# One TensorE branch per gate, up and down matrix, and weight splits of 2048 columns in three buffers

## The chip, the cores and the metric

The kernel runs on one core of one Trainium2 chip. The metric is the device time of one execution in microseconds (us). Three runs of the kernel before gave 1469.05, 1475.29 and 1476.32 us; their median is 1475.29 us.

## The reference: what is computed

A two-layer transformer trunk in float32: 256 tokens, width 1024. Each layer has a hybrid token mixer (latent attention, retention and block-sparse attention, fed by one input projection and joined by one output projection) and a channel mixer, each followed by a layer norm with a scaled residual. The channel mixer of layer 0 is a dense SwiGLU of width 2816. That of layer 1, on which this change works, is a mixture of eight SwiGLU experts with two experts for each token:

```python
logits = xt @ w_router
top_v, top_i = lax.top_k(logits, 2)
top_w = softmax(top_v)
gates = sum(one_hot(top_i, 8) * top_w[..., None], axis=1)
for e in range(8):
    y = y + gates[:, e:e+1] * (silu(xt @ w_gate[e]) * (xt @ w_up[e])) @ w_down[e]
```

Per expert, gate and up are 1024 x 3584 and down is 3584 x 1024, all float32. The weights of the eight experts are 352 MB, and all of them are read in every execution.

## The kernel before, in words

**Precision by splits.** TensorE works on a reduced float32 (F32R). Each weight tile is split into a high part `whi` (ScalarE's cast, line 152) and a low part `wlo` (VectorE's subtraction, line 153; for five early splits partly on GpSimd), and each product is three matmuls: high by high, high by low, low by high (`mm3`, lines 162 to 164). `split` makes one pair for up to 1024 columns, in a pool of `SPL` = 5 buffers for `whi` and 5 for `wlo` that lives through the whole kernel.

**Raw weights.** SyncE's queue loads the weights in pieces of 128 x 2048 (1 MB, line 122). In the expert stage `mchunk` takes the pieces' buffers from three pools in the cyclic order `ORDER`: 12 of them, and one more early piece (`EARLY`) in a buffer that a later gather uses. A load is issued when its buffer is free, that is, when VectorE has done the subtraction on what was there.

**The expert stage** goes over expert e = 0 to 7 and, in each, over m = 0 to 6, 56 blocks in all. A block multiplies the tokens of the expert (at most 128 slots, gathered by matmuls) by 512 columns of gate and of up, and 512 rows of down. The order on TensorE is: gate of this block, transposes of the hidden rows `hh` of the block before (`turn`), up of this block, down of the block before. Gate, up and down are 4096 columns each, so each is four splits of 1024.

**Heavy and light.** From expert 1 on, the count of the expert's tokens decides at run time. With more than 64 tokens the block runs `heavy`: three matmuls per product. With 64 or fewer it runs `light`: the high and the low part of the tokens stand side by side in the 128 columns of the stationary operand, so two matmuls do, and the two halves of the result are folded together by one more matmul (`fold`, line 838). For the fold, ScalarE first copies the bank to `fl` (line 850). `either` writes this as an If with an Else on TensorE alone. Before the change each of gate, up and down has two such branches, one per two splits, and the folds are Ifs of their own (`folded`, line 837): one after the first half of up (for gate) and one after the first half of the next down (for up). So a block has eight Ifs. Expert 0 has none, it is always heavy.

**What is put between the splits.** `defer(n, fn)` runs `fn` after n more splits of 1024: the copy to `fl` (`FOLD_N`), ScalarE's silu on the gate bank (line 894, `SILU_N`), the high and low part of the transposed rows (`halves`, lines 922 and 924, `HT_N`) and VectorE's product of silu and up (line 900, `MULT_N`). Within that, the framework's scheduler orders the instructions of each engine ahead of time, by when it thinks that they are ready, so a deferred one may stand a few splits later in its engine's queue than in the program. Each engine then works through its queue in order.

**Before the first expert.** `hold_splits` gives the first splits of expert 0 to VectorE or GpSimd and ties them behind certain instructions of the layer norm and the router, so that five splits are made while the router runs.

Of the kernel before, what the change touches and what calls it, by code (L numbers as in the profile page):

```python
# [18 lines left out]
P = 128  # L19
D = 1024  # L20
# [14 lines left out]
EARLY = 12  # L35
# [9 lines left out]
ORDER = (0, 0, 0, 0, 1, 1, 1, 1, 1, 0, 0, 2)  # L45
LAST = (7, 6)
POOL_LO = ()
# [40 lines left out]
def trunk(ctx: ExitStack, tc: tile.TileContext, x, consts, mconsts, vecs, lnrows, w_in, w_uq, w_ukv, w_o,  # L88
# [5 lines left out]
    spl = ctx.enter_context(tc.tile_pool(name="spl", bufs=SPL))  # L94
# [543 lines left out]
    def moe(pool, raws2, raws3, r, gb, rw):  # L638
# [4 lines left out]
        def mchunk(src, parts=1):  # L643
            pools = []
            for _ in range(2):
                i = nchunk[0]
                nchunk[0] += 1
                pools.append((pool, "xg") if i == EARLY else (raws, raws2, raws3)[ORDER[(i - (i > EARLY)) % 12]])
            return chunk(src, 4096, pools=pools, parts=parts)
# [76 lines left out]
        def gather(pr):  # L726
            pm = pool.tile([P, 2, 256], F32R, tag="pm", name="pm")
            for tt in range(2):
                for j in range(2):
                    ip = nc.vector.tensor_scalar(pm[:, tt, j * P:(j + 1) * P], iota, posm[:, tt, 2 * pr + j:2 * pr + j + 1],  # L730
                                            None, ALU.is_equal)
            if pr == 0:
                hold_splits(((), None, 2), ((pw,), nc.gpsimd, 2), ((i1, pw), nc.gpsimd, 1), ((i1, ip), None, 4))
            xgs = [pool.tile([P, KD, P, 2], F32R, tag="xg", name="xg", bufs=3) for j in range(2)]

            def part(k2):
                for hl, src in enumerate((xth, xtl)):
                    b = bank(acc, "gx")
                    for kk in range(2):
                        k = 2 * k2 + kk  # L740
                        for tt in range(2):
                            nc.tensor.matmul(b[:, kk * 256:(kk + 1) * 256], src[:, tt, k * P:(k + 1) * P], pm[:, tt, :],
                                             start=(kk == 0 and tt == 0), stop=(kk == 1 and tt == 1))
                    bv = b.rearrange("p (a b) -> p a b", b=256)
                    for j in range(2):
                        o = xgs[j][:, 2 * k2:2 * k2 + 2, :, hl]
                        if j == 0:
                            nc.vector.tensor_copy(o, bv[:, :, 0:P])
                        else:
                            nc.scalar.copy(o, bv[:, :, P:256])  # L750

            return pm, xgs, part
# [45 lines left out]
        nsplit = [0]  # L798

# [5 lines left out]
        def msplit(src):  # L805
            i_ = nsplit[0]
            nsplit[0] += 1
            pool_lo = i_ % 12 in POOL_LO
            t = split(src, 1024, nc.gpsimd if pool_lo else nc.vector)
            if not pool_lo:  # L810
# [24 lines left out]
        def folded(e, b, fl):  # L835
            if few[e] is not None:
                with tc.If(few[e] != 0):  # L837
                    nc.tensor.matmul(b, fold, fl[0], start=False, stop=True, skip_group_check=True)

        def gate_up(e, m, xg, part=None, mid=None):  # L840
# [3 lines left out]
            if part:  # L844
                part(0)

            def copy_for_fold(g, fl):
                with after(last[0]):
                    fl.append(pool.tile([P, 512], F32R, tag="fl", name="fl"))
                    nc.scalar.copy(fl[0], bs[g])  # L850

            fls = [[], []]
            for g, w in enumerate((e_gate, e_up)):
                raw = mchunk(w[e, m], 2 if g == 1 and (e, m) == LAST else 1)
                for q in range(2):
                    if part and g == 0:
                        sp = []
                        for k in range(4 * q, 4 * q + 4):
                            if k % 2 == 0:
                                if k < 6:  # L860
                                    part(k // 2 + 1)
                                sp.append(msplit(raw(k * 512, 1024)))
                            cs = slice((k % 2) * 512, (k % 2 + 1) * 512)
                            mm3(bs[g], xg[:, k, :, 0], xg[:, k, :, 1], sp[-1][0][:, cs], sp[-1][1][:, cs], k == 0, k == 7)
                        continue
                    sp = [msplit(raw(k * 512, 1024)) for k in (4 * q, 4 * q + 2)]
                    parts_ = [(k, sp[k // 2 % 2][0][:, k % 2 * 512:k % 2 * 512 + 512],
                               sp[k // 2 % 2][1][:, k % 2 * 512:k % 2 * 512 + 512]) for k in range(4 * q, 4 * q + 4)]

                    def heavy():  # L870
                        for k, hi, lo in parts_:
                            mm3(bs[g], xg[:, k, :, 0], xg[:, k, :, 1], hi, lo, k == 0, k == 7)

                    def light():
                        for k, hi, lo in parts_:
                            x2 = xg[:, k, 0:64, :].rearrange("p a b -> p (a b)")
                            nc.tensor.matmul(bs[g], x2, hi, start=(k == 0), stop=False)  # L877
                            nc.tensor.matmul(bs[g], x2, lo, start=False, stop=(k == 7))  # L878

                    either(e, heavy, light)  # L880
                    if g == 1 and q == 0:
                        folded(e, bs[0], fls[0])
                if dyn:
                    if g == 0 or (e, m) != LAST:
                        defer(FOLD_N, lambda g=g: copy_for_fold(g, fls[g]))
                    else:
                        copy_for_fold(g, fls[g])
                if g == 0:
# [7 lines left out]
                    defer(SILU_N, silu)  # L896
# [5 lines left out]
            def fold_up():  # L902
                folded(e, bs[1], fls[1])
                if (e, m) == LAST:
                    mult()
# [5 lines left out]
            return hh, fold_up  # L911
# [20 lines left out]
        def down(e, m, ht, yb, fold_up=None, hook=None):  # L932
            raw = mchunk(e_down[e, m], 2 if e == NE - 1 and m >= FM - 2 else 1)
            for q in range(2):
                sp = [msplit(raw(j * D, D)) for j in (2 * q, 2 * q + 1)]

                def heavy():
                    for j in (2 * q, 2 * q + 1):
                        hi, lo = sp[j % 2]
                        for n in range(2):  # L940
                            cs = slice(n * 512, n * 512 + 512)
                            mm3(yb[n], ht[:, j, 0], ht[:, j, 1], hi[:, cs], lo[:, cs], m == 0 and j == 0, m == FM - 1 and j == 3)

                def light():
                    for j in (2 * q, 2 * q + 1):
                        h2 = ht[:, j].rearrange("p a b -> p (a b)")[:, 0:256:2]
                        for n in range(2):
                            for i in range(2):
                                nc.tensor.matmul(yb[n], h2, sp[j % 2][i][:, n * 512:n * 512 + 512],  # L949
                                                 start=(m == 0 and j == 0 and i == 0), stop=(m == FM - 1 and j == 3 and i == 1))  # L950

                either(e, heavy, light)
                if q == 0 and fold_up:
# [111 lines left out]
        def finish(e, m, ht, fold_up=None, hook=None):  # L1065
# [3 lines left out]
            down(e, m, ht, yb[e], fold_up, hook)  # L1069
# [5 lines left out]
        for e in range(NE):  # L1075
            pr = e // 2
            for m in range(FM):
# [11 lines left out]
                hh, fold_up = gate_up(e, m, half[pr][1][e % 2], half[0][2] if e == 0 and m == 0 else None, mid)  # L1089
# [5 lines left out]
                if prev is not None:  # L1095
                    h2 = [ht[0]]
                    finish(*prev[:2], ht[0], fold_up, (lambda: h2.append(turn(hh, 0, 1024))) if (e, m) == LAST else None)
# [29 lines left out]
    with tc.tile_pool(name="pre", bufs=1, reuse_waits="tile") as pre:  # L1127
# [112 lines left out]
    with tc.tile_pool(name="moe", bufs=1, reuse_waits="tile") as mp, tc.tile_pool(name="raws3", bufs=ORDER.count(2), reuse_waits="tile") as raws3, \  # L1240
# [114 lines left out]
```

## Time and profile before

| what | value |
|---|---|
| median of three runs | 1475.29 us |
| the profiled execution, its own time | 1477.69 us |
| span of the profiled execution, first to last instruction | 1475.7 us |
| granted TensorE clock, mean | 0.981 of full speed |
| busy share of the span: TensorE, VectorE, ScalarE, GpSimd | 94%, 82%, 70%, 5% |
| read from HBM | 426.76 MB |
| expert stage, from about 487 to 1465 us: TensorE, VectorE, ScalarE busy | 918.8, 889.9, 791.9 of 978 us |

The shares are means over stages with different limits. Matmuls are pipelined, so two that follow one another overlap in the records: the distance between their starts is the cost of one, and a busy TensorE may still have room. An instruction's idle time and what ended it stand in brackets behind it; where a wait had several causes, the one named is the one that came last.

### The profile page before, as it was taken

To read this page: it belongs to the slowest core of one execution; us is meant where nothing else is said; L and a number is where in the kernel's file an instruction comes from. 1 tells how busy PE (TensorE), PEld (TensorE's weight loads), DVE (VectorE), ACT (ScalarE), POOL (GpSimd) and SP (SyncE) were. 2 spreads that over 40 slices of the span, in tenths; PEclk is the share of its full clock that TensorE was granted. 3 is DMA by queue.
4 is the path that set the end of the run, shared out by engine and by line. 5 is a ranking of instruction groups with operands and counts; after the bars stand their busy time and mean duration, and the time that the engine had idled before them with its cause. 6 is when DMAs were issued, how large, how long until landed. Compare 5 with 4: busy or idle time off the path is not lost. (4 is left out here: it accounts for less than half of the span.)

```text
span 1475.7 us, 20166 instructions
## 1 busy us (share of the span) xinstructions
PE 1379.9 (94%) x6927; PEld 1115.9 (76%) x6927; DVE 1204.0 (82%) x1590; ACT 1035.0 (70%) x1391; POOL 76.4 (5%) x113
## 2 busy tenths in 40 slices
PE   7999999999998999989889999998999999999995
PEld 6987999998986888766666677776677877777663
DVE  6577655547668799899999988899998888888997
ACT  3564444444655677878979877788887777778894
POOL 3112000003104000000000000000000000000001
PEclk8999999999998899999999999999999999999998
DMA  6733555544527599999999998989999898889980
GB/s 245 282 143 114 200 178 194 181 164 141 208 94 306 195 340 367 356 359 348 421 373 406 417 343 316 347 332 396 414 376 341 324 346 306 333 347 359 355 349 31
DMA packets 63526, 429.59 MB, mean 291 GB/s; under 512 B 7058, under 2 KB 7570, under 8 KB 15268
## 3 DMA queue, kind: packets, MB, share of 16 engines
q1 hardware_dynamic: 63364, 427.81, 75.9%
q8 instruction: 84, 1.38, 0.4%
q14 instruction: 46, 0.38, 0.1%
q0 software_dynamic: 32, 0.03, 0.0%
HBM read 426.76 MB, written 1.05 MB: 290 GB/s over the span
## 5 line engine op out<-in xcount | busy, mean ns | idle before, releaser
L153 DVE TENSOR_TENSOR wlo<-raw,whi 128x1024 fp32r<-128x1024 f32 (+3 forms) x801 | 933.7, 1213 | 156.7 <-ACT whi L152 155.1
L152 ACT CAST whi<-raw 128x1024 fp32r<-128x1024 f32 (+4 forms) x808 | 808.9, 1042 | 216.6 <-PE gu L586 44.0
L878 PE MATMUL eg<-wlo,xg 128*128 128x512 f32 x448 | 186.5, 416 | 1.8 <-DVE wlo L153 1.5
L162 PE MATMUL eg<-whi,xg 128*128 128x512 f32 x448 | 180.5, 403 | 6.8 <-PEq L837 6.8
L877 PE MATMUL eg<-whi,xg 128*128 128x512 f32 x448 | 180.3, 402 | 0.1
L163 PE MATMUL eg<-wlo,xg 128*128 128x512 f32 x448 | 176.9, 395 | 2.0 <-DVE wlo L153 1.7
L164 PE MATMUL eg<-whi,xg 128*128 128x512 f32 x448 | 176.0, 393 | 0.0
L878 PEld LDWEIGHTS eg<-wlo,xg 128*128 128x128 f32 x448 | 84.5, 189 | 50.1 <-DVE wlo L153 33.4
L162 PEld LDWEIGHTS eg<-whi,xg 128*128 128x128 f32 x448 | 87.3, 195 | 29.3 <-issue 12.8
L949 PE MATMUL y<-wlo,wk 128*128 128x512 f32 x224 | 96.7, 432 | 12.7 <-DVE wlo L153 12.6
L163 PEld LDWEIGHTS eg<-wlo,xg 128*128 128x128 f32 x448 | 87.4, 195 | 18.2 <-DVE wlo L153 3.8
L164 PEld LDWEIGHTS eg<-whi,xg 128*128 128x128 f32 x448 | 87.4, 195 | 16.0
L585 PE MATMUL gu<-xhi,whi 128*128 128x256 f32 x352 | 99.3, 282 | 0.1
L586 PE MATMUL gu<-xlo,whi 128*128 128x256 f32 x352 | 99.2, 282 | 0.2 <-DVE xlo L225 0.2
L587 PE MATMUL gu<-xhi,wlo 128*128 128x256 f32 x352 | 98.9, 281 | 0.0
L877 PEld LDWEIGHTS eg<-whi,xg 128*128 128x128 f32 x448 | 85.0, 190 | 15.9 <-issue 1.1
L949 PE MATMUL y<-whi,wk 128*128 128x512 f32 x224 | 93.3, 417 | 3.1 <-DVE wk L924 2.2
L162 PE MATMUL y<-whi,wk 128*128 128x512 f32 x224 | 90.2, 403 | 5.1 <-PEq L837 4.2
L163 PE MATMUL y<-wlo,wk 128*128 128x512 f32 x224 | 88.8, 396 | 1.6 <-DVE wlo L153 1.5
L164 PE MATMUL y<-whi,wk 128*128 128x512 f32 x224 | 88.5, 395 | 0.0
L949 PEld LDWEIGHTS y<-wlo,wk 128*128 128x128 f32 x224 | 45.1, 201 | 37.9 <-DVE wlo L153 31.7
L894 ACT ACTIVATE hh<-eg 128x512 f32<-128x512 f32 x56 | 33.6, 600 | 53.3 <-PEq L837 28.3
(307 smaller groups left out, 2147.3 us busy)
## 6 DMA issues: line engine op xcount, KB each, us to landing
raw<-in_e_gate SPq DMA_DIRECT2D x112, 1024.0 KB, 6.7
raw<-in_e_up SPq DMA_DIRECT2D x110, 1024.0 KB, 6.8
raw<-in_e_down SPq DMA_DIRECT2D x108, 1024.0 KB, 6.4
raw<-in_ffn_gu SPq DMA_DIRECT2D x22, 1024.0 KB, 4.9
raw<-in_ffn_dn SPq DMA_DIRECT2D x11, 1024.0 KB, 4.6
raw<-in_w_in SPq DMA_DIRECT2D x10, 960.0 KB, 4.6
raw<-in_w_o SPq DMA_DIRECT2D x8, 1024.0 KB, 6.2
gb<-in_lnrows SPq DMA_DIRECT2D x8, 512.0 KB, 4.3
```

The costliest lines, as they stand in the source:

```text
L152: last[0] = nc.scalar.copy(hi[:, :n], src)
L153: last[1] = (eng or nc.vector).tensor_tensor(lo[:, :n], src, hi.bitcast(F32)[:, :n], ALU.subtract)
L162: nc.tensor.matmul(o, ahi, bhi, start=start, stop=False)
L163: nc.tensor.matmul(o, ahi, blo, start=False, stop=False)
L164: return nc.tensor.matmul(o, alo, bhi, start=False, stop=stop)
L585: nc.tensor.matmul(o, hi[:, cs], xhi[:, k, :], start=(g == 0 and k == 0), stop=False)
L586: nc.tensor.matmul(o, hi[:, cs], xlo[:, k, :], start=False, stop=False)
L587: nc.tensor.matmul(o, lo[:, cs], xhi[:, k, :], start=False, stop=(g == 1 and k == 7))
L877: nc.tensor.matmul(bs[g], x2, hi, start=(k == 0), stop=False)
L878: nc.tensor.matmul(bs[g], x2, lo, start=False, stop=(k == 7))
L894: nc.scalar.activation(hh, bs[0], AF.Silu)
L949: nc.tensor.matmul(yb[n], h2, sp[j % 2][i][:, n * 512:n * 512 + 512], start=(m == 0 and j == 0 and i == 0), stop=(m == FM - 1 and j == 3 a ...
```

## The change

`either` is now called once for gate, once for up and once for down, after both of its splits are issued. The fold of gate goes into the light branch of up, before its last two products, and the fold of up into the light branch of down, before its last row block; where that down belongs to the expert before (m = 0), the fold of up keeps an If of its own. `msplit` makes splits of 2048 columns, in a new pool `spl2` of three buffers that opens with the expert stage, where the pool of five is closed. The first block, the last up and the last two downs still work in instructions of 1024 columns. The raw buffers are 11 instead of 12 and the early piece is the 12th instead of the 13th. Silu and the product of an expert with a branch wait for one more split (of 1024, counted). The last product of silu and up moves from behind its fold to behind the down that contains it.

```diff
-EARLY = 12
+EARLY = 11
-ORDER = (0, 0, 0, 0, 1, 1, 1, 1, 1, 0, 0, 2)
+ORDER = (0, 0, 0, 0, 1, 1, 1, 1, 0, 0, 2)
...
-    def split(src, n, lo_eng=None):
-        hi = spl.tile([P, 1024], F32R, tag="whi", name="whi")
-        lo = spl.tile([P, 1024], F32R, tag="wlo", name="wlo")
+    spl = [None]
+
+    def split(src, n, lo_eng=None, to=None):
+        hi, lo = to or [spl[0].tile([P, 1024], F32R, tag=t, name=t) for t in ("whi", "wlo")]
...
-                hold_splits(((), None, 2), ((pw,), nc.gpsimd, 2), ((i1, pw), nc.gpsimd, 1), ((i1, ip), None, 4))
+                hold_splits(((), None, 2), ((pw,), nc.gpsimd, 2), ((i1, pw), nc.gpsimd, 1), ((i1, ip), None, 3))
...
+        def msplit(raw, o, halves=False, before=None):
+            t = [spl[0].tile([P, 2048], F32R, tag=x, name=x) for x in ("whi", "wlo")]
+            n = 1024 if halves else 2048
+            for c in range(0, 2048, n):
+                if before:
+                    before((o + c) // 1024)
+                split(raw(o + c, n), n, nc.vector, [x[:, c:c + n] for x in t])
                 dve[0] = last[1]
-            for q in list(later):
-                q[0] -= 1
-                if q[0] == 0:
-                    later.remove(q)
-                    q[1]()
+                for q in list(later):
+                    q[0] -= n // 1024
+                    if q[0] <= 0:
+                        later.remove(q)
+                        q[1]()
             return t
...
-        def folded(e, b, fl):
-            if few[e] is not None:
-                with tc.If(few[e] != 0):
-                    nc.tensor.matmul(b, fold, fl[0], start=False, stop=True, skip_group_check=True)
+        def fold_in(b, fl):
+            if fl:
+                nc.tensor.matmul(b, fold, fl[0], start=False, stop=True, skip_group_check=True)
...
+                def four(q):
+                    halves = (e, m) == (0, 0) or g == 1 and (e, m) == LAST
+                    sp.append(msplit(raw, q * 2048, halves, (lambda i: i < 3 and part(i + 1)) if part and g == 0 else None))
+
+                def light():
+                    for k in range(KD):
+                        if g == 1 and k == 6:
+                            fold_in(bs[0], fls[0])
+                        cs = slice(k % 4 * 512, k % 4 * 512 + 512)
+                        x2 = xg[:, k, 0:64, :].rearrange("p a b -> p (a b)")
+                        nc.tensor.matmul(bs[g], x2, sp[k // 4][0][:, cs], start=(k == 0), stop=False)
+                        nc.tensor.matmul(bs[g], x2, sp[k // 4][1][:, cs], start=False, stop=(k == 7))
+
+                if dyn:
+                    four(0)
+                    four(1)
                     either(e, heavy, light)
-                    if g == 1 and q == 0:
-                        folded(e, bs[0], fls[0])
+                else:
+                    for q in range(2):
+                        four(q)
+                        heavy(range(4 * q, 4 * q + 4))
...
-                    defer(SILU_N, silu)
+                    defer(SILU_N + dyn, silu)
...
-                defer(MULT_N, mult)
+                defer(MULT_N + dyn, mult)
...
+            if few[e] is not None:
+                sp.extend(msplit(raw, q * 2048, parts > 1) for q in range(2))
                 either(e, heavy, light)
-                if q == 0 and fold_up:
+            else:
+                for q in range(2):
+                    sp.append(msplit(raw, q * 2048, parts > 1))
+                    heavy((2 * q, 2 * q + 1))
+            if fold_up and fe != e and few[fe] is not None:
+                with tc.If(few[fe] != 0):
                     fold_up()
...
+                    def hook():
+                        mult()
+                        h2.append(turn(hh, 0, 1024))
...
-    with tc.tile_pool(name="pre", bufs=1, reuse_waits="tile") as pre:
+    with tc.tile_pool(name="spl", bufs=SPL, reuse_waits="tile") as spl[0], \
+            tc.tile_pool(name="pre", bufs=1, reuse_waits="tile") as pre:
...
+    with tc.tile_pool(name="spl2", bufs=3, reuse_waits="tile") as spl[0], \
+            tc.tile_pool(name="moe", bufs=1, reuse_waits="tile") as mp, tc.tile_pool(name="raws3", bufs=ORDER.count(2), reuse_waits="tile") as raws3, \
             tc.tile_pool(name="raws2", bufs=ORDER.count(1), reuse_waits="tile") as raws2:
```

## Rows read from the trace of the kernel before

**Rows 1.** Windows, one block each: stretch, us, busy (count) per engine, PEclk, DMA, GB/s.

```profile
554.90:572.10 17.20, 17.20 (x78) 14.29 (x77) 15.68 (x15) 13.48 (x14) 0.00 (x0) 1.00 0.96 366
...
929.90:948.20 18.30, 17.67 (x77) 14.06 (x76) 15.13 (x15) 13.95 (x17) 0.00 (x0) 1.00 0.91 340
...
1306.70:1325.00 18.30, 17.67 (x80) 14.11 (x78) 15.26 (x15) 14.08 (x17) 0.00 (x0) 1.00 0.87 342
...
1046.20:1061.10 14.90, 14.29 (x56) 9.15 (x55) 14.90 (x15) 13.47 (x18) 0.00 (x0) 1.00 1.01 417
1407.90:1422.80 14.90, 14.29 (x57) 9.17 (x56) 14.90 (x15) 13.48 (x17) 0.00 (x0) 1.00 1.01 411
```

**Rows 2.** The page's costliest groups: count, busy us, mean ns, idle before and its releaser.

```profile
L878 PE MATMUL eg<-wlo,xg 128*128 128x512 f32 x448 | 186.5, 416 | 1.8 <-DVE wlo L153 1.5
L162 PE MATMUL eg<-whi,xg 128*128 128x512 f32 x448 | 180.5, 403 | 6.8 <-PEq L837 6.8
```

**Rows 3.** Waits of SyncE's DMA queue: us in total, times, longest.

```profile
SPq L122 <- DVE wlo L153: 1036.1, 370, 18.6
```

**Rows 4.** Timeline around the end of a heavy up's first half, all engines.

```profile
1181.27 0.40 PE L164 MATMUL eg<-whi,xg 128*128 128x512 f32 x1
1181.80 0.60 ACT L894 ACTIVATE hh<-eg 128x512 f32<-128x512 f32 x1 [1.82 <-PEq L837]
...
1181.98 0.50 PE L162 MATMUL eg<-whi,xg 128*128 128x512 f32 x1 [0.32 <-PEq L837]
...
1182.33 0.40 PE L163 MATMUL eg<-wlo,xg 128*128 128x512 f32 x1
```

**Rows 5.** TensorE's timeline where that up ends and the down's branch begins.

```profile
1184.64 0.40 PE L164 MATMUL eg<-whi,xg 128*128 128x512 f32 x1
1184.87 0.40 PE L162 MATMUL y<-whi,wk 128*128 128x512 f32 x1
```

**Rows 6.** What stands on line 837 (the fold's If): count, ns min/median/max, first and last.

```profile
L837 PEldq EVENT_SEMAPHORE  x42: 51/51/51, 841.5 to 1339.7; - x42
```

**Rows 7.** Groups by form before 480 us: splits of 1024 and 640 columns.

```profile
L153 DVE TENSOR_TENSOR wlo<-raw,whi 128x1024 fp32r<-128x1024 f32 x94 | 114.7, 1225 | 76.2 <-ACT whi L152 76.2
...
L153 DVE TENSOR_TENSOR wlo<-raw,whi 128x640 fp32r<-128x640 f32 x10 | 8.2, 818 | 1.4 <-ACT whi L152 1.4
...
L152 ACT CAST whi<-raw 128x1024 fp32r<-128x1024 f32 x97 | 101.4, 1048 | 89.9 <-PE gu L586 44.0 <-PE fo L164 19.9 <-issue 16.0
...
L152 ACT CAST whi<-raw 128x640 fp32r<-128x640 f32 x10 | 7.3, 728 | 6.4 <-DVE wlo L153 3.3 <-PE pf L273 2.2 <-ACT pr L402 0.5
```

**Rows 8.** Timelines of VectorE and of ScalarE in a light block.

```profile
802.03 9.16 DVE L153 TENSOR_TENSOR wlo<-raw,whi 128x1024 fp32r<-128x1024 f32 x8
811.11 0.68 DVE L924 TENSOR_TENSOR wk<-ht,wk 128x512 fp32r<-128x512 f32 x1
811.78 4.63 DVE L153 TENSOR_TENSOR wlo<-raw,whi 128x1024 fp32r<-128x1024 f32 x4
...
810.21 0.60 ACT L894 ACTIVATE hh<-eg 128x512 f32<-128x512 f32 x1 [1.43 <-PE eg L838]
810.70 3.88 ACT L152 CAST whi<-raw 128x1024 fp32r<-128x1024 f32 x4
```

**Rows 9.** VectorE's timeline in the heavy block of rows 4.

```profile
1183.36 4.63 DVE L153 TENSOR_TENSOR wlo<-raw,whi 128x1024 fp32r<-128x1024 f32 x4 [2.66 <-ACT whi L152]
```

**Rows 10.** Before the experts: VectorE's timeline, and TensorE's last matmuls of the output projection.

```profile
453.90 1.23 DVE L153 TENSOR_TENSOR wlo<-raw,whi 128x1024 fp32r<-128x1024 f32 x1 [0.47 <-ACT whi L152]
...
468.47 5.57 DVE L202 SCALAR_TENSOR_TENSOR r<-t,sums,gb 128x512 f32<-128x512 f32 x2 [1.40 <-POOL sums L195]
...
L163 PE MATMUL wo<-wlo,mhi x64: 390/394/398, 118.1 to 463.4; 128*128 128x512 f32 x64
```

**Rows 11.** Timelines of VectorE and of TensorE at the end of the expert stage.

```profile
1450.90 0.68 DVE L900 TENSOR_TENSOR hh<-eg,hh 128x512 f32<-128x512 f32 x1
...
1454.60 0.70 PE L949 MATMUL y<-whi,wk 128*128 128x512 f32 x1 [2.16 <-DVE wk L924]
```

**Rows 12.** The page's queue of instruction fetches: packets, MB, share of 16 engines.

```profile
q8 instruction: 84, 1.38, 0.4%
```

More of the change, by code (lines that the diff above doesn't have):

```diff
@@ L845, in gate_up, with copy_for_fold @@
                 part(0)
-            def copy_for_fold(g, fl):
+            fls = [[], []]
+            def copy_for_fold(g):
                 with after(last[0]):
-                    fl.append(pool.tile([P, 512], F32R, tag="fl", name="fl"))
-                    nc.scalar.copy(fl[0], bs[g])
-            fls = [[], []]
+                    fls[g].append(pool.tile([P, 512], F32R, tag="fl", name="fl"))
+                    nc.scalar.copy(fls[g][0], bs[g])
             for g, w in enumerate((e_gate, e_up)):
@@ L854, in gate_up @@
                 raw = mchunk(w[e, m], 2 if g == 1 and (e, m) == LAST else 1)
[L855 to L878, printed above, removed]
@@ new lines, in gate_up, with heavy @@
+                sp = []
+                def four(q):
+                    halves = (e, m) == (0, 0) or g == 1 and (e, m) == LAST
+                    sp.append(msplit(raw, q * 2048, halves, (lambda i: i < 3 and part(i + 1)) if part and g == 0 else None))
+                def heavy(ks=range(KD)):
+                    for k in ks:
+                        cs = slice(k % 4 * 512, k % 4 * 512 + 512)
+                        mm3(bs[g], xg[:, k, :, 0], xg[:, k, :, 1], sp[k // 4][0][:, cs], sp[k // 4][1][:, cs], k == 0, k == 7)
@@ L886, in gate_up @@
                     else:
[L887 removed]
+                        copy_for_fold(g)
                 if g == 0:
@@ L930, in turn, with down, heavy, light @@
             return ht
[L932 to L950, printed above, removed]
-                either(e, heavy, light)
-                if q == 0 and fold_up:
+        def down(e, m, ht, yb, fold_up=None, fe=None, hook=None):
+            parts = 2 if e == NE - 1 and m >= FM - 2 else 1
+            raw = mchunk(e_down[e, m], parts)
+            sp = []
+            def heavy(js=range(4)):
+                for j in js:
+                    for n in range(2):
+                        cs = slice(j % 2 * D + n * 512, j % 2 * D + n * 512 + 512)
+                        mm3(yb[n], ht[:, j, 0], ht[:, j, 1], sp[j // 2][0][:, cs], sp[j // 2][1][:, cs], m == 0 and j == 0, m == FM - 1 and j == 3)
+            def light():
+                for j in range(4):
+                    if j == 3 and fold_up and fe == e:
+                        fold_up()
+                    h2 = ht[:, j].rearrange("p a b -> p (a b)")[:, 0:256:2]
+                    for n in range(2):
+                        for i in range(2):
+                            nc.tensor.matmul(yb[n], h2, sp[j // 2][i][:, j % 2 * D + n * 512:j % 2 * D + n * 512 + 512],
+                                             start=(m == 0 and j == 0 and i == 0), stop=(m == FM - 1 and j == 3 and i == 1))
+            if few[e] is not None:
+                sp.extend(msplit(raw, q * 2048, parts > 1) for q in range(2))
+                either(e, heavy, light)
+            else:
[4 more added lines that the diff above has]
+                with tc.If(few[fe] != 0):
@@ L1087, in mid @@
                         ht[0] = turn(prev[2], HT_N)
-                hh, fold_up = gate_up(e, m, half[pr][1][e % 2], half[0][2] if e == 0 and m == 0 else None, mid)
+                hh, fold_up, mult = gate_up(e, m, half[pr][1][e % 2], half[0][2] if e == 0 and m == 0 else None, mid)
                 if e == 0 and m == 0:
```

27 lines of the change are left out of this document (7 added, 20 removed).

## The prediction

> **What bounds the kernel now.** I read the page's slices first: the expert stage is two thirds of the span, so I cut it into windows of one block each [rows 1]. There are three kinds. A block of expert 0, always heavy and without branches, takes 17.2 us with TensorE busy throughout. A heavy block behind branches takes 18.3 us, and there TensorE alone is short of the window, by 0.6 us. A light block takes 14.9 us, and there VectorE is busy for all of it. The counts of the matmul groups say how many of each [rows 2]: 16 matmuls of line 162 per heavy block and 16 of line 878 per light one, so 448 of each are 28 heavy blocks (7 of expert 0, 21 behind branches) and 28 light ones. The transfers bound nothing yet: SyncE's queue waits for VectorE to free raw buffers [rows 3]. In light blocks they run at 411 to 417 GB/s with the engines always busy [rows 1], so they are not far behind.
>
> Then the timeline of a heavy block, for the 0.6 us. Matmuls follow one another every 0.23 us. Where the first half of up ends, the next one starts 0.71 us after the last, and the one behind it 0.35 us later [rows 4]. That is 0.48 + 0.11 = 0.59 us lost. Where up ends and the branch of down begins, the distance is 0.23 us: an If with an Else costs nothing [rows 5]. The difference is the fold's own If. A heavy block doesn't take it, and on that way a semaphore instruction stands: 42 of them, 21 blocks times 2 [rows 6]. I read the gap as TensorE having to finish before it can give that signal. The check is that 2 x 0.59 = 1.18 us is the difference of the two kinds of heavy block, 18.3 - 17.2 = 1.1.
>
> **The change part by part.**
>
> *The fold's Ifs.* In the new heavy branch there is no fold, so no untaken If. Only the fold of up at m = 0 keeps one, once for each of the three heavy experts behind branches. 42 - 3 = 39 gaps of 0.59 us go, all on TensorE where TensorE sets the time: 39 x 0.59 = -23.0 us. Bounds: 0, if the buffers below take it back, and -25 (21 x 1.2, if a heavy block comes down to 17.1 us). The other four Ifs per block that go are worth 0 by rows 5.
>
> *Splits of 2048.* Back to back, eight subtractions take 9.16 us [rows 8] and one takes 1.22 us [rows 7], so each further one costs (9.16 - 1.22) / 7 = 1.13 us. From 640 to 1024 columns the duration grows by (1225 - 818) / 384 = 1.06 ns a column [rows 7], so one of 2048 is 1.22 + 1.09 = 2.31 us alone and 2.22 us back to back, against 2.27 us for two: 0.05 us saved. Six per block and 28 light blocks give -8.4 us. For a cast the same working gives (1048 - 728) / 384 = 0.83 ns a column, 1.90 us alone and 1.80 us back to back against 1.89. In heavy blocks VectorE has room, so it counts nothing there.
>
> [...]
>
> *Three buffers instead of five.* Columns in buffers rise from 5120 to 6144, but TensorE now holds 2048 of them at a time, and a fill takes 1.90 + 2.31 = 4.2 us instead of 2.3. No row shows three buffers, so I follow one block by hand. Heavy, from the end of gate on TensorE at 0: transposes until 0.35 (17.2 us less 72 x 0.233), then 2.80 us per split (12 matmuls): up ends at 5.95, down at 11.55. The tight place is the next gate's first split. ScalarE gets its buffer at 5.95, but first has silu and the copy to `fl`, which both wait for the end of up (0.2 us for the branch's end, about 0.5 us each): cast from 7.1 to 9.0, subtraction to 11.3. TensorE wants it at 11.55: 0.25 us of slack. Light, from VectorE's end with up at 0: TensorE ends up at 2.2 (8 matmuls, a fold, the tail); silu 0.49, `fl` 0.48, cast 1.90, ready at 5.1. VectorE wants it after the transposed rows and two splits, 0.67 + 2 x 2.22 = 5.1: no slack. So the light blocks keep half of their 8.4, -4, and the heavy ones lose a little, +5 (0.25 us in 21 blocks). Bounds: 0 to +25 in the heavy blocks, -8 to +14 in the light ones (half a microsecond each). Ten blocks have a scatter or a gather as well, where engines wait for one another already: +3 (0 to +10).
>
> *The wait of silu.* It waits for the end of up, not of its first half. What stands behind it in ScalarE's queue waits as well. Now that is the casts of down: silu waits 1.82 us and then the casts start [rows 4], VectorE is idle for 2.66 us [rows 9], and five buffers keep it from TensorE. I count 0 here, because the change puts silu one split later, and take the other order as a rival.
>
> *Eleven raw buffers.* One megabyte less is 2.4 us less lead at 417 GB/s, of some 29 us in all. I take 0; it costs only if transfers become the bound.
>
> *Start and end.* Expert 0's first subtractions run at 453.90, in VectorE's idle time [rows 10]. The new pool lies over the old one, whose last tiles TensorE reads until 463.4 [rows 10]. If the first buffer has to wait for that, two subtractions of 1.13 us land in the layer norm's chain: 0 to +2.3, taken as +1.2. A subtraction on GpSimd there slows VectorE already (two additions in 5.57 us), but that happens before and after alike. At the end the last product of silu and up starts at 1450.90 [rows 11] and waits for nothing but VectorE. Now it stands behind the whole down, about four matmuls and a branch's end later, +1 (0 to +1.5), because TensorE idles there until 1454.60 [rows 11].
>
> *Sum.* -23.0 - 4 + 5 + 3 + 1.2 + 1 = -16.8 us, so the profiled execution's 1477.7 us becomes 1460.9. The median of the runs shown is 2.4 us below that execution, so I forecast 1458.5 us; the forecast's own range is 1450 to 1468.
>
> **The rivals.**
>
> *A cast behind silu* (slower). If silu and the copy to `fl` stand ahead of the cast of down's second split in ScalarE's queue, as a cast stands behind silu now, that cast starts after up has ended: in a heavy block at 7.1, ready at 11.3, wanted at 8.75, 2.55 us late; in a light one ready at 5.1, wanted at 2.89, 2.2 us late. In all blocks that is 21 x 2.55 + 28 x 2.2 = 115 us against 31 won: about 1560. It decides from some 13 of the 49 blocks on. For it: rows 4 and 9. Against: silu is asked for one split later, and a cast whose buffer comes free at 3.15 is ready before it.
>
> *Three buffers are too few.* A slack of 0.25 us is gone with one more instruction in the way. If each of the 49 blocks loses 0.6 us, 29 us stand against the 23 won, and with the start, the end and the scatters the time is 1475 to 1487, say 1480. For it: no slack in the chain of a light block. Against: the slack is positive in the heavy ones, where the gain is.
>
> *Everything fits.* Both gains are kept and the start costs nothing: -23 - 8.4 + 1, 1445. For it: ScalarE may take the next gate's cast ahead of silu, which leaves the light blocks slack. Against: transfers then need 6.29 MB per 14.6 us, 431 GB/s, which rows 1 never show; the lead carries that for some blocks.
>
> *Longer jumps.* A light block now jumps over 24 matmuls and their weight loads, not 12. If each of the 63 branches of the heavy blocks waited for a fetch of instructions, 0.4% of 16 engines' span over 84 packets [rows 12] or 1.1 us each, that would be +69 us, some 1527. Against: rows 5 show nothing at a jump over a body. [...]
>
> **How the numbers follow.** Forecast 0.48, too few buffers 0.22, everything fits 0.17, a cast behind silu 0.10, longer jumps 0.03. A change of 0.5% (7.4 us) is about what a measurement of this kernel can tell from none. Faster: 0.45 of the forecast and 0.17, 0.62. Same: 0.03 of the forecast and 0.09 of the buffers, 0.12. Slower: 0.13 of the buffers and 0.13 of the last two, 0.26. The range, 1440 to 1488, takes in the first three cases and leaves the last two out.
>
> **What would show it.** Three semaphore instructions are left at the fold's If instead of 42, no start distance of 0.71 us within a heavy block's up and down, and the heavy blocks of experts 3, 5 and 6 at 17.2 to 17.5 us. Light blocks at 14.6 to 14.9 us, with subtractions 2.22 us apart. In ScalarE's queue, casts of down ahead of silu. Wrong would be idle time of TensorE before low parts in heavy blocks, idle time of VectorE before casts in light ones, or a time over 1468.

## The result: 1.0% slower, and the profile after

The changed kernel takes 1487.64 us (median of 4 runs, 1486.29 to 1489.02), the kernel before 1472.24 us (median of 4). The ratio is 1.0103, 95% interval 1.0069 to 1.0137. The forecast was 1458.5 us. The profiled execution's span is 1486.9 us, 11.3 more than before.

The windows of the changed kernel, one block each (columns as in [rows 1]): a heavy block, a light one, a heavy block with a gather, and the first block of a heavy expert.

```profile
938.90:956.20 17.30, 17.27 (x79) 14.07 (x77) 14.66 (x9) 13.26 (x11) 0.00 (x0) 1.00 0.97 362
...
1031.80:1046.30 14.50, 13.10 (x54) 9.47 (x54) 14.45 (x9) 12.90 (x11) 0.00 (x0) 1.00 1.01 417
...
894.30:921.60 27.30, 22.67 (x107) 18.84 (x105) 17.92 (x21) 16.01 (x19) 0.00 (x0) 0.94 0.71 267
835.60:852.70 17.10, 16.01 (x70) 12.83 (x69) 14.45 (x9) 13.31 (x13) 0.00 (x0) 1.00 1.01 418
```

And the gather's block of the same expert before:

```profile
890.30:911.50 21.20, 20.73 (x105) 17.26 (x104) 17.93 (x22) 15.90 (x23) 0.00 (x0) 1.00 0.80 298
```

The steady blocks did what was forecast: heavy ones went from 18.3 to 17.3 us with TensorE full, light ones from 14.9 to 14.5 with VectorE full [rows 1]. The gather's block went from 21.2 to 27.3 us, and there no engine is full: TensorE is busy for 22.67 us.

The groups of the light and of the heavy gate and up count 448 again [rows 2]: as many blocks of each kind. From the page's groups:

```profile
L871 PE MATMUL eg<-wlo,xg 128*128 128x512 f32 x448 | 182.5, 407 | 11.6 <-DVE wlo L152 9.5
```

SyncE's queue still waits for VectorE [rows 3]:

```profile
SPq L120 <- DVE wlo L152: 1037.1, 367, 20.6
```

Instruction fetches stay at 0.4% [rows 12]:

```profile
q8 instruction: 81, 1.33, 0.4%
```

On the one fold If that is left, 3 semaphore instructions stand instead of 42 [rows 6]:

```profile
L954 PEldq EVENT_SEMAPHORE  x3: 51/51/51, 847.1 to 1234.9; - x3
```

ScalarE's timeline in the heavy block above, and VectorE's in the light one:

```profile
948.03 1.91 ACT L151 CAST whi<-raw 128x2048 fp32r<-128x2048 f32 x1 [0.69 <-PE eg L162]
949.84 0.59 ACT L892 ACTIVATE hh<-eg 128x512 f32<-128x512 f32 x1
...
1039.57 6.69 DVE L152 TENSOR_TENSOR wlo<-raw,whi 128x2048 fp32r<-128x2048 f32 x3
```

Here silu follows a cast and waits for nothing (it waited 1.82 us in [rows 4], and VectorE 2.66 us behind it in [rows 9]). Three subtractions take 6.69 us, the last of them 2.29, so they start 2.20 us apart; 2.22 was worked out from [rows 7, 8].

Before the stage, the output projection's last such matmul starts at 466.2 instead of 463.4 us [rows 10]:

```profile
L162 PE MATMUL wo<-wlo,mhi x64: 388/389/628, 118.6 to 466.2; 128*128 128x512 f32 x64
```

At the end the product stands behind seven subtractions, and TensorE's transposes wait for it [rows 11]:

```profile
1461.74 0.68 DVE L898 TENSOR_TENSOR hh<-eg,hh 128x512 f32<-128x512 f32 x1
...
1462.47 0.65 PE L166 MATMUL ht<-mc,hh 128*128 128x128 f32 x4 [3.01 <-DVE hh L898]
```

The start of each block's first gate matmul, taken from the two traces, shows where the 11.3 us arise (us; m = 0 and 1 are the first two blocks of experts 1 to 7, and the block m = 1 holds the scatter of the expert before):

| | start | expert 0 | 7 at m=0 | 7 at m=1 | 3 gathers | 13 steady heavy | 18 steady light | rest | span |
|---|---|---|---|---|---|---|---|---|---|
| before | 487.9 | 117.0 | 111.1 | 147.0 | 60.1 | 239.5 | 275.1 | 38.0 | 1475.7 |
| after, difference | +2.3 | +1.6 | +9.0 | +1.5 | +18.8 | -11.3 | -12.6 | +2.0 | +11.3 |

So 24 us were won in 31 steady blocks, and 35 lost around them, 18.8 of them in three blocks.

### The profile page after: what moved, and what is told of

It is laid out like the page before. It is cut to its first block, busy times and chain, and to the rows that moved or that the text cites. A ratio compares the mean times of both kernels' runs of the same rounds, so it can differ in the third digit from the quotient of the medians.

```text
span 1486.9 us, 18580 instructions
## 1 busy us (share of the span) xinstructions
PE 1368.8 (92%) x6927; PEld 1131.7 (76%) x6927; DVE 1177.1 (79%) x1264; ACT 994.1 (67%) x1065; POOL 79.8 (5%) x113
## 3 DMA queue, kind: packets, MB, share of 16 engines
HBM read 426.76 MB, written 1.05 MB: 288 GB/s over the span
## 5 line engine op out<-in xcount | busy, mean ns | idle before, releaser
L152 DVE TENSOR_TENSOR wlo<-raw,whi 128x2048 fp32r<-128x2048 f32 (+4 forms) x475 | 910.3, 1937 | 170.5 <-ACT whi L151 164.9
L151 ACT CAST whi<-raw 128x2048 fp32r<-128x2048 f32 (+4 forms) x482 | 772.3, 1619 | 295.3 <-PE eg L163 45.5
L943 PE MATMUL y<-wlo,wk 128*128 128x512 f32 x224 | 95.7, 427 | 11.3 <-DVE wlo L152 10.0
L161 PEld LDWEIGHTS eg<-whi,xg 128*128 128x128 f32 x448 | 88.3, 197 | 16.7
L585 PE MATMUL gu<-xlo,whi 128*128 128x256 f32 x352 | 99.7, 283 | 0.2 <-DVE xlo L224 0.2
L943 PE MATMUL y<-whi,wk 128*128 128x512 f32 x224 | 91.3, 407 | 2.8 <-DVE wk L917 1.5
L161 PE MATMUL y<-whi,wk 128*128 128x512 f32 x224 | 88.2, 395 | 0.3 <-ACT hh L892 0.3
L163 PE MATMUL y<-whi,wk 128*128 128x512 f32 x224 | 88.2, 394 | 0.0
L584 PEld LDWEIGHTS gu<-xhi,whi 128*128 128x128 f32 x352 | 67.6, 192 | 0.7 <-DVE xlo L224 0.3
```

The costliest lines, as they stand in the source:

```text
L161: nc.tensor.matmul(o, ahi, bhi, start=start, stop=False)
L163: return nc.tensor.matmul(o, alo, bhi, start=False, stop=stop)
L584: nc.tensor.matmul(o, hi[:, cs], xhi[:, k, :], start=(g == 0 and k == 0), stop=False)
L585: nc.tensor.matmul(o, hi[:, cs], xlo[:, k, :], start=False, stop=False)
L943: nc.tensor.matmul(yb[n], h2, sp[j // 2][i][:, j % 2 * D + n * 512:j % 2 * D + n * 512 + 512], start=(m == 0 and j == 0 and i == 0), stop= ...
```

## The experiments

Theory A: the gathers' blocks pay because the splits have no lead there, that is, none is ready ahead of the time at which TensorE wants it (three buffers of 2048, two of them held by the matrix in work). Rival B: the whole-matrix branch itself is the cost, as it leaves the gather's eight groups only three places per block. Later the question was which part of the change pays and which costs. "Before" is 1475.4 to 1476.5 us beside the runs below and was 1472.24 beside the changed kernel, so a difference from the changed kernel can be off by some 4 us. Ratios are to before; block differences are against the table's first row.

**One part at a time.** Large branches with splits of 1024 in five buffers:

```diff
-spl2: bufs=3 x 2048      11 raw buffers
+spl2: bufs=5 x 1024      12 raw buffers   (whole-matrix branches stay)
```

> The change's one branch per matrix alone: splits stay at 1024 columns in five buffers, 12 raw buffers, as before. Theory A (the loss sits in the gather blocks because a copy there now stands behind 2048-column splits, with three buffers and so no lead): the folds' own Ifs are gone, so steady heavy blocks take 17.3 us as in the changed kernel, steady light ones 14.9 as before, the gather blocks 17 to 21 us as before; some 1455 to 1465 us, faster than before. Rival B (the loss sits there because TensorE's branch now holds a whole matrix, so that the gather's eight groups are taken up later): the gather blocks keep 24 us (light expert) and 27 us (heavy), the light blocks lose the splits' gain of 12.5 us; some 1485 to 1500 us.

1573.84 us, ratio 1.067 (1.0641 to 1.0698): 98 us slower, worse than either theory said, and in steady blocks too (heavy 18.3, light 16.5 to 16.7 us). TensorE's transposes wait in every steady heavy block:

```profile
981.60 0.66 PE L166 MATMUL ht<-mc,hh 128*128 128x128 f32 x4 [0.96 <-DVE hh L897]
```

A branch holds four of the five buffers. Neither theory had that number in it.

Splits of 2048 in three buffers, with two branches per matrix and the folds in their own Ifs:

```diff
-    four(0); four(1); either(e, heavy, light)
+    for q in range(2): four(q); either(e, heavy(q), light(q)); fold in its own If
```

> The change's splits alone: 2048 columns in three buffers, 11 raw buffers, but two branches per matrix and the folds in Ifs of their own, as before. Theory A (coarse splits with three buffers cost the gather blocks): gather blocks 24 us (light) and 27 us (heavy) as in the changed kernel, steady heavy blocks 18.3 us, steady light ones 14.6; some 1490 to 1505 us. Rival B (the whole-matrix branch costs them): gather blocks 17 to 21 us as before, heavy 18.3, light 14.6; some 1460 to 1470 us.

1528.85 us, ratio 1.0367 (1.0342 to 1.0393). The gathers' blocks are near before's (16.5, 23.5, 23.3 us), which spoke for B; but the steady heavy blocks take 19.8 us, which neither had. There silu waits for the fold's If, and casts of 2048 columns stand behind it:

```profile
945.97 0.60 ACT L889 ACTIVATE hh<-eg 128x512 f32<-128x512 f32 x1 [2.31 <-PEq L836]
```

So large branches alone and large splits alone are each worse than the whole: they lean on each other.

**The gather.** Its groups spread over four blocks, two in each:

```diff
-if m == 3 and e % 2 == 1: gather, parts 0 to 3 at once
+if 2 <= m <= 5 and e % 2 == 1: one half of part m - 2 after gate and up, the other after down
```

> The changed kernel, with the eight groups of each gather (pairs 1 to 3) spread over four blocks, two in each, instead of all in one. If the loss is a burst of copies that come one behind the other, each behind a large split (A and B alike), two groups in a block find slack: the three gather blocks lose most of their extra 18.7 us and the blocks beside them gain little, some 1468 to 1477 us. Rival C (each group costs its wait wherever it stands, 0.8 us or so): the time stays at 1485 to 1495 us.

1476.01 us, ratio 1.0007 (0.9991 to 1.0022), at the edge of the expected range: about 12 us come back, and rival C falls. The three blocks lose 25 us, the blocks beside them take 11 more. A light block with two groups still takes 17.5 us; ScalarE's copy waits there for VectorE's [3.87 <-DVE xg L748].

Only the instructions cut to 1024 in the blocks around a gather:

```diff
-halves = first or last block
+halves = first or last block or (e odd, m in (3, 4))
```

> The changed kernel with every split cut to 1024 columns in the blocks 3 and 4 of the experts that hold a gather (and the down projections done there); the buffers stay three of 2048 columns, the branches one per matrix. Theory A in its first form (a copy of the gather waits behind one long instruction): the gather blocks fall by 10 us or more in all, 1470 to 1478 us. If it is the buffers or the branch and not the length of an instruction, no gain: 1485 to 1492 us.

1508.89 us, ratio 1.0225 (1.02 to 1.025). Blocks of 28.5, 30.9 and 32.6 us: A's first form, one long instruction in the way, falls; in this kernel shorter ones made it worse.

**Copies on ScalarE**, in the changed kernel and in the spread one:

```diff
-if j == 0: nc.vector.tensor_copy(...)   else: nc.scalar.copy(...)
+nc.scalar.copy(...)   for both, pairs 1 to 3
```

> The changed kernel with both copies of each gathered bank (pairs 1 to 3) on ScalarE, instead of one on VectorE and then one on ScalarE. If the five groups that TensorE issues one behind the other lose their time because ScalarE waits for VectorE's copy, which stands behind 2.24-us subtractions: the three gather blocks fall by 3 to 6 us each, in all 1470 to 1478 us. If they lose it because five groups stand in one place and there are few banks: 1484 to 1490 us.

> The gather's groups spread over four blocks, and both copies of each on ScalarE. In the first spread kernel a light block with two groups took 17.5 us beside 14.6 without, with ScalarE waiting up to 3.9 us for VectorE's copy. If that wait is the cost: such light blocks fall to about 15 us, the heavy ones (18.3 us, TensorE full) stay, in all 1460 to 1468 us. If not: 1474 to 1480 us.

1485.25 us (1.0067, 1.0048 to 1.0086), about what one place for five groups would give, and 1501.77 us (1.0156, 1.0126 to 1.0186), a clear miss. The second shows the mechanism. ScalarE and then TensorE in a heavy block:

```profile
933.16 0.67 ACT L750 CAST xg<-gx 128x256 fp32r<-128x256 f32 x2 [4.70 <-PE gx L742]
933.70 1.91 ACT L151 CAST whi<-raw 128x2048 fp32r<-128x2048 f32 x1
...
937.99 0.51 PE L162 MATMUL eg<-wlo,xg 128*128 128x512 f32 x1 [1.82 <-DVE wlo L152]
```

A group's copy waits for TensorE to finish the whole gate and issue the group; the cast for up's second half stands behind the copy in the queue; TensorE, done with the first half, waits for that split. So the wait for VectorE's copy isn't all that costs: with both copies on ScalarE, a copy in front of a split without lead costs more still.

**The folds alone.** Before, with the folds at the end of the half-matrix branches that were there:

```diff
                         light: matmuls of this half
+                        if g == 1 and q == 0: fold_in(bs[0], fls[0])      (down likewise)
-                    if g == 1 and q == 0: folded(e, bs[0], fls[0])
```

> The kernel before with one thing of the change: the folds of the light experts stand at the end of the half-matrix branches that were there, so their own Ifs go (one is left at the first block of each expert); splits of 1024 in five buffers, 12 raw buffers and two branches per matrix stay. If the folds' untaken Ifs cost TensorE's time as forecast (about 1 us in a heavy block), steady heavy blocks go from 18.3 to 17.3 us, light ones stay at 14.9 (VectorE is busy 98% of those), the gather blocks stay at 17 to 21 us: some 1455 to 1463 us. If the heavy blocks' gain in the changed kernel came from its large branches or splits instead: 1470 to 1476 us.

1454.03 us (1451.83 to 1456.51), ratio 0.986 (0.9839 to 0.9882): 22 us faster than before, and no kernel here was measurably faster. The windows of a steady heavy, a steady light and a gather's block:

```profile
918.80:935.90 17.10, 17.10 (x77) 14.23 (x76) 15.08 (x15) 14.01 (x17) 0.00 (x0) 1.00 0.97 369
1017.70:1032.50 14.80, 14.16 (x56) 9.14 (x54) 14.80 (x15) 13.60 (x17) 0.00 (x0) 1.00 1.02 421
879.10:901.70 22.60, 21.41 (x109) 18.16 (x108) 18.97 (x27) 16.62 (x25) 0.00 (x0) 1.00 0.82 307
```

What is left on the fold's If:

```profile
L837 PEldq EVENT_SEMAPHORE  x3: 51/51/51, 840.8 to 1207.4; - x3
```

**The same columns in small buffers.** Whole-matrix branches with six buffers of 1024:

```diff
-spl2: bufs=3 x 2048
+spl2: bufs=6 x 1024      (11 raw buffers, as in the changed kernel)
```

> One branch per matrix with splits of 1024 columns, but in six buffers (as many columns as the changed kernel's three of 2048) and 11 raw buffers. If the 98 us that one branch per matrix with five buffers cost over before came of the missing buffer (a branch's matrix holds four of five): steady heavy blocks 17.3 us, light ones 14.9, gather blocks 25 to 31 us, in all 1490 to 1515 us. If the length of the instructions matters instead of the buffers: it stays at 1560 to 1580 us.

1461.74 us, ratio 0.9911 (0.9891 to 0.993), below the expected range: 112 us under five buffers and 26 under the changed kernel, with the same branches and the same three places for the gather's groups. B falls as the cause of the loss. The gather's block, to be held against 27.30 us (and 22.60 with half branches and the folds inside):

```profile
887.00:909.80 22.80, 21.40 (x109) 18.04 (x108) 14.46 (x19) 12.66 (x19) 0.00 (x0) 1.00 0.79 301
```

TensorE's timeline of four groups on end, 2.64 us from the first to the next matrix:

```profile
900.75 0.63 PE L741 MATMUL gx<-pm,xth 128*128 128x256 f32 x4
901.22 0.64 PE L741 MATMUL gx<-pm,xtl 128*128 128x256 f32 x4
902.32 0.73 PE L741 MATMUL gx<-pm,xth 128*128 128x256 f32 x4 [0.46 <-ACT xg L749]
902.89 0.66 PE L741 MATMUL gx<-pm,xtl 128*128 128x256 f32 x4
903.39 0.40 PE L161 MATMUL y<-whi,wk 128*128 128x512 f32 x1
```

In the changed kernel five groups take 6.18 us (905.96 to 912.14) in the same place, with the clock down behind them. TensorE's timeline:

```profile
905.96 0.63 PE L741 MATMUL gx<-pm,xth 128*128 128x256 f32 x4
906.42 0.64 PE L741 MATMUL gx<-pm,xtl 128*128 128x256 f32 x4
907.53 0.74 PE L741 MATMUL gx<-pm,xth 128*128 128x256 f32 x4 [0.46 <-ACT xg L749]
910.58 0.91 PE L741 MATMUL gx<-pm,xtl 128*128 128x256 f32 x4 [2.32 <-ACT xg L749]
911.29 1.06 PE L741 MATMUL gx<-pm,xth 128*128 128x256 f32 x4
912.14 0.63 PE L161 MATMUL y<-whi,wk 128*128 128x512 f32 x1
```

The windows of that stretch and of what follows:

```profile
906.00:912.20 6.20, 3.42 (x22) 3.01 (x21) 3.94 (x5) 5.11 (x7) 0.00 (x0) 0.90 0.63 251
912.20:915.50 3.30, 3.30 (x12) 2.59 (x11) 2.62 (x2) 1.04 (x3) 0.00 (x0) 0.67 0.87 300
```

VectorE's and TensorE's timeline at the end of that block:

```profile
919.37 0.42 DVE L747 CAST xg<-gx 128x256 fp32r<-128x256 f32 x1 [4.36 <-PE gx L741]
919.71 0.73 DVE L784 TENSOR_SCALAR pm<-mc,gt 128x64 fp32r<-128x64 f32 x4
920.35 0.68 DVE L898 TENSOR_TENSOR hh<-eg,hh 128x512 f32<-128x512 f32 x1
...
921.18 0.63 PE L166 MATMUL ht<-mc,hh 128*128 128x128 f32 x4 [1.85 <-DVE hh L898]
```

VectorE sits 4.36 us before the copy of the last group, which TensorE issues only after the whole of down. The product that TensorE needs next stands behind it.

**The size of a buffer.** The changed kernel with all splits cut to 1024, in its three buffers of 2048:

```diff
-halves = first or last block
+halves = True      (bufs=3 x 2048 stays)
```

> The changed kernel with every split of the expert stage cut to 1024 columns, but its buffers still three of 2048; so it differs from the run with six buffers of 1024 (1461.7 us) in nothing but how many columns come free at a time. If the size of the buffers is the cause (a cast can't start before TensorE is done with 2048 columns, and all of the spare third buffer is one matrix half ahead): gather blocks of 28 to 32 us as in the run that cut them there alone, time 1505 us or more. If the length of the instructions is the cause: gather blocks 19 to 23 us, 1460 to 1468 us.

1550.04 us, ratio 1.0514 (1.0496 to 1.0531). Beside the run with six small buffers the program differs in the number of columns that come free at a time (and in one split before the first expert): 88 us. A gather's block takes 32.5 us, a steady heavy one 18.0, a light one 16.5:

```profile
918.90:951.40 32.50, 23.84 (x109) 19.50 (x108) 18.92 (x27) 16.63 (x25) 0.00 (x0) 0.89 0.56 205
970.90:988.90 18.00, 17.26 (x78) 14.05 (x77) 15.14 (x15) 13.70 (x17) 0.00 (x0) 1.00 0.93 353
1077.96:1094.44 16.48, 13.48 (x56) 10.77 (x55) 14.71 (x15) 13.27 (x16) 0.00 (x0) 0.91 1.01 401
```

ScalarE's longest wait for a buffer in a steady heavy block, here and with six small buffers:

```profile
974.65 2.00 ACT L151 CAST whi<-raw 128x1024 fp32r<-128x1024 f32 x2 [2.89 <-PE eg L163]
947.08 2.00 ACT L151 CAST whi<-raw 128x1024 fp32r<-128x1024 f32 x2 [1.52 <-PE eg L162]
```

The two kernels' queues aren't in the same order, though: the scheduler put casts, copies and products at other places among the splits (with six small buffers a cast stands between the high part of the rows and the copy to `fl`, here none does). So the 88 us are those of the buffers together with the order that was made for them. The run is also 62 us over the changed kernel, though the buffers are the same; there deferred work lands in other places among the splits as well, so that difference isn't settled.

**A fourth large buffer:**

```diff
-spl2: bufs=3 x 2048, 11 raw buffers
+spl2: bufs=4 x 2048,  9 raw buffers
```

> The changed kernel with four split buffers of 2048 columns, paid for with two raw buffers (9 instead of 11). If the lead of the splits over TensorE is what the gather blocks lack: 20 to 23 us instead of 24 to 27, blocks at an expert's start 1 us less each, some 1455 to 1470 us unless nine raw buffers make ScalarE wait for loads. If the cause is the place of the gather's groups between only three branches: 1483 to 1490 us.

1471.03 us, ratio 0.9971 (0.9954 to 0.9988): 16.6 us under the changed kernel, a little above the expected range. The gathers' blocks fall to 16.6, 24.8 and 24.7 us, steady ones to 17.1 and 14.4. ScalarE's longest group of waits for a buffer between 825 and 1320 us, for five small, three large, six small and four large (us, times, longest):

```profile
ACT whi L151 <- PE eg L162: 51.2, 14, 6.2
```
```profile
ACT whi L151 <- PE eg L163: 25.7, 11, 3.1
```
```profile
ACT whi L151 <- PE eg L162: 24.6, 17, 1.5
```
```profile
ACT whi L151 <- PE eg L162: 7.1, 3, 3.4
```

With six small buffers this group is as long as with three large ones, but no wait in it is over 1.5 us. All of ScalarE's waits for TensorE to free a buffer in this stretch add up to 99.7, 81.6, 33.3 and 10.6 us. The run with four large ones has two raw buffers fewer as well.

**Branch size and small terms.** Six small buffers with two branches per matrix; then, from the kernel with the folds inside, the raw buffer, the pool, and a spread gather by themselves:

```diff
 e10: folds inside half branches, spl2: bufs=6 x 1024, 11 raw buffers
 e14: folds inside half branches, 11 raw buffers instead of 12
 e15: folds inside half branches, split pool closed and opened anew for the experts
 e13: folds inside half branches, gather spread as above
```

> Folds inside the branches, two branches per matrix, and six buffers of 1024 columns with 11 raw buffers: beside the run with one branch per matrix and the same six buffers (1461.7 us) it shows what the large branch itself costs or gives, beside the run with five buffers and two branches (1454.0 us) what the sixth buffer gives. If a branch of a whole matrix costs by itself (its splits must all be there before it begins): 1445 to 1455 us. If it gives (two Ifs fewer for each matrix pair): 1462 to 1470 us.

> The kernel with the folds inside its half-matrix branches (1454.0 us), with 11 raw buffers instead of 12. The prediction priced the twelfth raw buffer at nothing: 1452 to 1456 us. The rival: it is part of the 14.8 us by which the run with 11 raw buffers, six split buffers and a split pool of the expert stage's own was slower: 1458 to 1468 us, with light blocks of uneven length.

> The kernel with the folds inside its half-matrix branches (1454.0 us), 12 raw buffers and five split buffers as it has, but the split pool closed ahead of the expert stage and opened anew, as the change does to make its buffers larger. If that is what makes the expert stage's first gate matmul 2 to 6 us later in every kernel with it (490 us against 483 to 488): 1456 to 1460 us, all of it ahead of 490 us. If not: 1452 to 1456 us.

> The kernel with the folds inside its half-matrix branches (1454.0 us; five buffers of 1024), with the gather's groups spread over four blocks as in the first spread kernel. If a gather in one block is dear only where split buffers are large, spreading gains nothing here: 1452 to 1462 us. If spreading helps whatever the buffers: 1442 to 1449 us.

| | us | ratio to before, 95% |
|---|---|---|
| six small, two branches | 1468.83 | 0.996 (0.9944 to 0.9975) |
| 11 raw buffers | 1456.57 | 0.9871 (0.9852 to 0.9891) |
| own pool | 1459.14 | 0.9885 (0.9867 to 0.9902) |
| spread gather | 1455.12 | 0.9852 (0.9836 to 0.9869) |

Given six small buffers, whole-matrix branches are 7.1 us faster than halves (1468.83 against 1461.74). Against the kernel with the folds inside (1454.03), the run without the raw buffer is 2.5 us slower and the one with its own pool 5.1, with intervals that overlap that kernel's, so neither is shown to cost. That leaves some 7 of the 14.8 us between that kernel and the first row of the table, which go with the sixth buffer, or with the three together; there light blocks vary from 13.6 to 17.8 us, and why wasn't found. Spreading the gather gives nothing with five small buffers and half branches: a gather costs as much there in four blocks as in one.

## Why the prediction was wrong

The block differences of three runs against before, from one profile each, to be read beside the changed kernel's row above (us):

| | start | expert 0 | 7 at m=0 | 7 at m=1 | 3 gathers | 13 steady heavy | 18 steady light | rest | span |
|---|---|---|---|---|---|---|---|---|---|
| folds inside | -4.6 | -0.3 | +3.8 | -7.2 | +5.8 | -16.7 | -10.0 | +3.3 | -25.8 |
| six small, one branch | +1.6 | +1.2 | +4.1 | -13.1 | +4.9 | -16.9 | -6.0 | +5.2 | -19.1 |
| four large | +3.4 | +0.5 | +6.4 | -1.2 | +6.0 | -16.8 | -10.0 | +4.1 | -7.7 |

- **The fold's Ifs (-23.0): right in kind, and the sum partly by luck.** By themselves they gave 22 us (1475.9 to 1454.03), and 39 of 42 went. That TensorE has to finish before the signal is the prediction's reading of the gap; no run shows it. The steady heavy blocks came down to the 17.1 us of the outer bound. But 10.0 us came from steady light blocks, where nothing was forecast (four of them had taken 16.9 to 18.2 us before and now took 13.2 to 14.8), and 7.2 from the second blocks, while the gathers' and the first blocks lost 9.6.
- **Splits of 2048 (-8.4 possible, -4 taken): about right.** Subtractions start 2.20 us apart (2.22 worked out), so a merged pair saves 2 x 1.13 - 2.20 = 0.06 us, and an ordinary light block takes 14.55 us instead of the 14.82 of the run with the folds inside: 0.27 us less, where 6 x 0.05 = 0.3 was possible. Of the 12.6 us that the 18 steady light blocks won, 10.0 are there without the large splits.
- **Three buffers in steady blocks (+5 heavy, no slack in light): about right.** An ordinary heavy block takes 17.32 us instead of some 17.1 with the folds inside, where 0.25 us was forecast. The 13 steady heavy blocks kept 0.87 us each, where (23.0 - 5) / 21 was 0.86.
- **"Ten blocks have a scatter or a gather as well ...: +3 (0 to +10)": the step that failed.** The three gathers cost +18.8 and the seven blocks with a scatter +1.5 against before, 20.3 us in all. Held against the run with the folds inside, where these blocks have the folds' gain as well, the term is 21.7 us: 13.0 in the gathers and 8.7 in the blocks with a scatter; against six small buffers it is 13.8 and 14.7. The slack of 0.25 us was worked out for a steady block only. A gather puts sixteen copies in the two queues through which every split goes, and a copy waits for a group that TensorE issues after a whole matrix (VectorE sat 4.36 us before one). The timelines above show such waits reaching TensorE where the one spare buffer holds 2048 columns; with four large buffers the gathers cost 12.8 us less than with three. The blocks with a scatter weren't followed: a fourth large buffer gives them back only 2.8 us, and why small buffers give so much more there stays open.
- **Not priced by itself: the first block of each expert, +9.0** for seven. It is +4.1 with six small buffers and +3.8 with the folds inside, so about 5 go with the large buffers.
- **Start (+1.2) and end (+1): +2.3 and +2.0.** Expert 0 took 1.6 more. The pool that is opened anew is part of the start: in a kernel with it and nothing else new, expert 0's first gate matmul comes at 489.7 us; in three that keep the old pool at 483.3, 487.7 and 487.8, so one profile each doesn't settle it.
- **Eleven raw buffers (0), silu (0): near enough.** The raw buffer's 2.5 us lie within overlapping intervals; ScalarE's casts of the expert stage now wait for a load five times, 10.3 us in all, and did not before. Silu waits seven times, 6.0 us in all, where it waited 52.8 us before.
- **Two slips in the working.** The 0.35 us for the transposes should be 17.2 - 72 x 0.233 = 0.42, which moves both ends of the slack alike, and a piece of 1.05 MB at 417 GB/s is 2.5 us of lead, not 2.4.
- **The rivals.** "Three buffers are too few" named the resource and came near in time (1480), but put the loss into all 49 blocks, and the steady ones gained. "A cast behind silu" and "Longer jumps" are excluded by the steady blocks, "Everything fits" by the others.

By the parts, the time goes 1475.9 (before), 1454.0 (folds inside), 1468.8 (six small buffers, own pool, 11 raw), 1461.7 (one branch per matrix), 1487.6 (three large buffers instead of six small). The last step took back more than the first gave; the forecast had the large splits and their three buffers together at some +4 (-4 + 5 + 3).

## What to carry to other kernels

Count buffers in what comes free at a time, less what the unit in work holds: six small ones and three large ones hold the same columns, and were 26 us apart. Check the slack of a new buffer plan in the irregular blocks (gathers, a change of expert), not only in the steady one: here a copy in front of a split without lead made TensorE, the bottleneck, wait (1.82 us in the spread kernel with both copies on ScalarE). And try the cheap part of a bundled change alone: here it won 22 us, and the rest of the bundle lost 34.

## What the hardware showed unexpectedly

In the gather of the changed kernel TensorE stood idle for 2.8 of 6.2 us. Its granted clock was 0.90 there and 0.67 in the next 3.3 us: 0.50 from 912.2 to 914.0 us, 1.00 from 914.5 to 915.5. Down's first matmuls started 0.43 us apart, those from 914.57 us on 0.23. The six before 914.57 took 2.43 us, where six at 0.23 take 1.4. The kernel with six small buffers kept 1.00 through its gather. In the run with small splits in large buffers the whole block had 0.89. So the stall in the gather, with the low clock behind it, cost some 1.0 us more than its own length.
